# Elementwise work with two SBUF inputs moved from GpSimd to VectorE in a hybrid recurrence and MLP step

## The chip, the cores and the metric

The kernel runs on one core of a Trainium2 chip. The metric is device time in microseconds (us) of one execution. The engines are called as in the profile: PE is TensorE's matrix multiply, PEld its weight load, DVE is VectorE, ACT is ScalarE, POOL is GpSimd, SP is SyncE, which here only issues DMAs. Each engine runs its own instructions in the order of the program and waits on semaphores for the others.

## The reference

One inference step of a diffusion backbone with two layers over 128 context and 1024 latent tokens (1152 together), model width 1024, all in float32:

```python
for i in range(2):
    sh1, sc1, gt1, sh2, sc2, gt2 = adaln(cond, ada_w[i], ada_b[i])      # silu(cond) @ w + b
    h = rmsnorm(x, norm_mix_g[i]) * (1 + sc1) + sh1
    o = hgrn2_mixer(h, ...) if i == 0 else chunk_mlp_mixer(h, ...)
    x = x + gt1 * o
    h = rmsnorm(x, norm_mlp_g[i]) * (1 + sc2) + sh2
    x = x + gt2 * (square(relu(h @ w1)) @ w2)                           # hidden width 4096
y = rmsnorm(x, final_norm_g)

def hgrn2_mixer(h, ...):      # per head, both directions, 8 heads of 128
    zq, zff, zfb, zi, zg = split(h @ w_in);  q = silu(zq);  v = zi
    f = lb + (1 - lb) * sigmoid(zf);  k = 1 - f
    # S_t = f_t * S_(t-1) + k_t v_t^T,  o_t = S_t^T q_t
    o = rmsnorm(o_forward + o_backward) * silu(zg);  return o @ w_out, final states

def chunk_mlp_mixer(h, ...):  # chunks of 128 tokens, 8 groups
    u, v = split(gelu(h @ w_in));  v = layernorm(v)
    s = w_s @ v + b_s          # over the positions of a chunk
    return (u * s) @ w_out
```

The outputs are y of both token groups and the final states of the recurrence.

## The kernel before, in words

Tokens lie in the free dimension, in three blocks of TB = 384; the model width is 8 tiles of 128 partitions (KD = 8). A float32 product is done as three matmuls on a faster float32 form: a high part of each operand and the rest ("low part"), high x high, high x low, low x high (`mm3`). The high part of a weight is a copy by ACT, the low part is raw minus high, a `tensor_tensor` with two SBUF inputs on DVE or POOL (`hi_lo`, L241; each weight names its engine). Names: `wraw` is the loaded weight (128x1024, by SP's queue, two buffers for it and `adav` together), `whi`/`wlo` and `wunit` its parts, `hh`/`hl`, `hidh`/`hidl`, `hc`, `oh`/`ol`, `uh`/`ul` those of activations. Low parts are put in a list `late` and issued by `flush()`, in most places at once; weights are split ahead of use by `w_ahead()`.

The program is written out in one order; nothing reorders it. Its stages in the profiled execution are roughly: input norm and adaLN (0 to 110 us), the recurrence (110 to 740), head 7 beside the first half of the output projection (740 to 850), the second half, the first MLP's first token block and adaLN's end (to 1150), its other two blocks with Winograd's seven products in place of eight (`quad`, 1150 to 1655), the gMLP mixer (1655 to 2025), the second MLP and the final norm (2025 to 2823).

*Recurrence.* The program interleaves two generators: `z_groups(h)` multiplies the input projection of head h in 15 steps, here called slots (five sections times three token blocks), and `gla_gen(h - 1)` does the recurrence of the head before. In slot 0 lie ks, K and Q, in slot 1 the products aps, in slots 2 to 8 the seven levels, in 9 and 10 the transposes ktp, in 11 and 12 the state updates S with the products ups, in 13 and 14 the outputs og from the products ops; the gated norm (orp) of a head follows in the next head's slots 0, 2 and 3. K = 1 - F stands before ks. A level multiplies K and Q by decays (`L964`, `L971`, `L972` on DVE), forms the pairwise products of the decays for the next level (`TT`, `L962`, on POOL), does the products lps on PE and merges them under a mask (`L974` on DVE). The next level's lps reads this level's Q.

*adaLN.* The rest of the first layer's adaLN is a product of a vector with a matrix on DVE, in steps (`ada_vec`, L375): a tile `adav` of 512 KB is loaded, and a step does four multiply-and-accumulate instructions over half of it. The load of the next tile is issued by the generator behind the last read of a tile. Of the ring of two buffers that it shares with `wraw`, adav uses one and the same buffer each time in the recurrence. In the recurrence one step stands in each of slots 2 to 6 and 9 to 14. Two steps per quarter of the matrix only fill `bc`.

*Squares.* For the norms ACT squares each tile (`sq_step`) and the squares are added into `acc`, nearly all on POOL (L436); ones-matmuls then sum over partitions (`ss`, `rms_a`), DVE takes the reciprocal root (`rq`), a matmul spreads it (`rp`), ACT copies it to SBUF (`rstd`).

*Winograd.* A weight tile pair is loaded and summed: one sum on DVE (L292, to PSUM), three on POOL (L293, L298, L299, `SUM_ENG`); their low parts are on DVE.

Of the kernel before, what the change touches and what calls it, by code (L numbers as in the profile page):

```python
# [19 lines left out]
KD = 8  # L20
# [18 lines left out]
def kernel(  # L39
# [95 lines left out]
    for h in range(8):  # L135
        for sect in (3, 0, 1, 2, 4) if h == 0 else (4, 3, 0, 1, 2):
            plain(w_in[sect * 8 + h], [KD, 128], nc.gpsimd)
    for part in range(2):
        for p in range(4):
            plain(w_out[part, p], [2, 4, 128], nc.gpsimd)  # L140

    # Winograd's form of the 2 x 2 x 2 block product, seven block products in place of eight.  A: w1 transposed,
    # in blocks of (hidden, model); B: the normed tokens, in blocks of (model, token block 1 or 2).
    # S1 = A21 + A22, S2 = S1 - A11, S3 = A11 - A21, S4 = A12 - S2
    # T1 = B12 - B11, T2 = B22 - T1, T3 = B22 - B12, T4 = B21 - T2
    # C11 = A11 B11 + A12 B21, U = A11 B11 + S2 T2, C12 = U + S1 T1 + S4 B22,
    # C22 = U + S3 T3 + S1 T1, C21 = U + S3 T3 + A22 T4
    W_SPLIT = ("A11", "A12", "S1", "S2", "S4", "S3", "A22")

    def mlp_specs(l):  # L150
# [5 lines left out]
        for part in range(1, 2):  # L156
            engs = (SUM_ENG, nc.vector)
            for b in range(8):
# [10 lines left out]
                def unit(p):  # L169
                    for n2 in range(1 if tail else 2):  # L170
                        at["u", 2 * p + n2] = len(items)
                        add_item("plain" if tail else "unit", (down[p],), n2, nc.gpsimd if tail else nc.vector)

# [17 lines left out]
    UP += [(1, n) for n in ("A12", "S2", "S4", "S3")] + [("u", 0), ("u", 1), (1, "A22")]  # L191
    SUM_ENG = nc.gpsimd
    P0_ENG = nc.vector

    mlp_specs(0)
    for half in range(2):
        for kp in range(4):
            plain(cw_v[half, kp], [2, 512], nc.gpsimd if half == 0 else nc.vector)
    for g in range(8):
        plain(cw_u[g], [KD, 128], nc.vector)  # L200
    for n in range(8):
        plain(cw_out[n], [KD, 128], nc.vector if n < 4 else nc.gpsimd)
    mlp_specs(1)
# [126 lines left out]
    def w_ahead(depth=None, most=2):  # L330
        d = depth if depth is not None else (3 if wextra else 1)
        n = 0
        while wst["split"] < wst["use"] + d and n < most and w_split():
            n += 1

    def mm3(ps, wh, wl, act, n, k0=0, k1=None):
        for k in range(k0, n if k1 is None else k1):
            ah, al = act(k)
            nc.tensor.matmul(ps, wh(k), ah, start=(k == 0), stop=False)  # L339
            nc.tensor.matmul(ps, wh(k), al, start=False, stop=False)  # L340
            nc.tensor.matmul(ps, wl(k), ah, start=False, stop=(k == n - 1))  # L341
# [80 lines left out]

    def sq_step(j, k, eng=None):
        xs = xtiles[k][:, tbs(j)]
        if j not in accs:
            acc = (wextra[0] if wextra and j == 1 else scr).tile([128, TB], F32, tag="acc", name="acc", bufs=1)
            nc.scalar.activation(acc, xs, AF.Square)
            accs[j] = acc
        else:
            p, tag, n = sq_pool  # L430
            sq = p.tile([128, TB], F32, tag=tag, name="sq", bufs=n)
            nc.scalar.activation(sq, xs, AF.Square)
            if eng == "last":
                accs[j] = (accs[j], sq)
                return
            (eng or nc.gpsimd).tensor_tensor(out=accs[j], in0=accs[j], in1=sq, op=ALU.add)  # L436

    rstds = {}

    rq = {}  # L440
    n4 = TB // 4

    def rms_a(j):
        ss = psum.tile([128, n4], F32, tag="n", name="ss", bufs=1)
        parts = accs.pop(j)
        parts = parts if isinstance(parts, tuple) else (parts,)
        for x, acc in enumerate(parts):
            for b in range(4):
                nc.tensor.matmul(ss[32 * b:32 * b + 32], ones_d, acc[:, b * n4:(b + 1) * n4],
                                 start=(x == 0), stop=(acc is parts[-1]))  # L450
        q = scr.tile([128, n4], F32, tag="rq", name="rq", bufs=1)
        nc.scalar.activation(q, ss, AF.Sqrt, bias=eps_sb[:, 0:1])
        nc.vector.reciprocal(q, q)
        rq[j] = q

    def rms_b(j, pool=None, tag="rstd"):
# [6 lines left out]
        nc.scalar.activation(r, rp, AF.Copy)  # L463
        rstds[j] = r

    H = {}
# [77 lines left out]
    def tail_groups(bodies, make_norm, per_step, lag, per_w, js=range(NTB), queue=()):  # L544
        queue = list(queue)
        for i, j in enumerate(js):
            for n, body in enumerate(bodies):
# [5 lines left out]
                for _ in range(per_step):  # L553
                    qstep(queue)
                if i == 0 and n < per_w or j == js[-1]:
                    w_ahead()
        queue.append(make_norm(js[-1]))
        return queue

    HC = {}  # L560
    C1_POOL = ("B11", "B22", "B21")
    ADA_PACE = (0.65, 0.72)
# [9 lines left out]
    def comb1(i):  # L572
# [6 lines left out]
        def put(n, q, t):  # L579
# [8 lines left out]
            HC[1, n, q] = w  # L588
            hi_lo(w, t, nc.gpsimd if n in C1_POOL else nc.vector, mine)

# [77 lines left out]
    with tc.manual_schedule():  # L668
# [18 lines left out]
        with tc.tile_pool(name="start", bufs=14, reuse_waits="tile") as sp:  # L687
# [43 lines left out]

            def squares(j, eng):
                for k in range(KD):
                    sq_step(j, k, eng)

            def norms(j, k0, k1, sq=()):
                for _, k in zip(norm_gen(0, j, False, k0, k1), list(sq) + [None] * KD):
                    if k is not None:
                        sq_step(2, k, nc.gpsimd if k < 6 else nc.vector)

# [13 lines left out]
            a_load(2)  # L754
            squares(0, nc.vector)
            rms_a(0)
# [12 lines left out]
            w0s[0] = w_next()  # L769
            squares(1, nc.vector)  # L770
            sbs = a_mm(2)
# [35 lines left out]
        with tc.tile_pool(name="gla", bufs=1, reuse_waits="tile") as gla:  # L807
# [14 lines left out]
            def z_groups(h):  # L822
# [60 lines left out]
                for sect, j in seq:  # L883
# [13 lines left out]
                    if (sect == 0 and j == 2 or sect == 4) if h == 0 else j == 0:  # L897
                        w_ahead()
                    yield st
# [5 lines left out]
            def gla_gen(h, st):  # L905
# [7 lines left out]
                for j in range(NTB):  # L913
                    eng = nc.vector if h == 7 else nc.gpsimd
                    eng.tensor_scalar(out=K[:, :, tbs(j)], in0=F[:, :, tbs(j)], scalar1=-1.0, scalar2=1.0,
                                            op0=ALU.mult, op1=ALU.add)
# [34 lines left out]
                for lev in range(7):  # L951
# [10 lines left out]
                    nc.gpsimd.tensor_tensor(out=cut(Tn, t0n, [[1, n]]), in0=cut(Tcur, t0c, [[2, n]]),  # L962
                                            in1=cut(Tcur, t0c + 1, [[2, n]]), op=ALU.mult)
                    nc.vector.tensor_tensor(out=kmix(hh), in0=kview(km, hh),  # L964
# [6 lines left out]
                    nc.vector.tensor_tensor(out=q0, in0=q0, in1=cut(Tcur, t0c + n + 1, [[2, nb], [0, hh]]), op=ALU.mult)  # L971
                    nc.vector.tensor_tensor(out=q1, in0=q1, in1=cut(Tcur, t0c, [[2, nb], [0, hh]]), op=ALU.mult)  # L972
                    if lev < 5:
                        nc.vector.copy_predicated(A32, mask_sb[:, lev:lev + 1, :].to_broadcast([128, NC, 32]), pss[0])  # L974
# [92 lines left out]
            def split_og(h, j):  # L1067
                oh = ptile("oh")
                ol = ptile("ol")
                split(oh, ol, ogt[h][:, tbs(j)], nc.vector if h % 2 else nc.gpsimd)  # L1070
                OG[h, j] = (oh, ol)

            def out_group(part, w, np_, n2, j):
                ps = zps("wops")
                mm_p(ps, w, n2, lambda k: OG[4 * part + k, j])
                resid(0, 2, 2 * np_ + n2, j, ps)

            spare = []
            ada = ada_vec0(lambda: spare[0] if slot % 15 < 7 else spare[1])
# [3 lines left out]
            for h in range(8):  # L1083
                for st in z_groups(h):
                    step(prev)
                    step(cur)
                    if h > 0 and slot % 15 in (2, 3, 4, 5, 6, 9, 10, 11, 12, 13, 14):
                        step(ada)
# [18 lines left out]
            for np_ in range(4):  # L1107
                w = w_next()
                for n2 in range(2 if np_ < 3 else 1):
                    for j in range(NTB):  # L1110
# [3 lines left out]
                        if j == 0 and n2 == 0:  # L1114
                            w_ahead()
                        step(prev)
                        if j < 2 or n2 == 0 and np_ > 0 or np_ == 2:
                            step(cur)
                        if np_ == 1 and n2 == 0:
                            for h in range(4, 7):  # L1120
# [38 lines left out]
        def mlp(l, pend, make_norm, yp, ada, early):  # L1159
# [15 lines left out]
            def product(part, q, name, w, tick):  # L1175
# [156 lines left out]
            def t_body(np_, n2):  # L1332
                def f(j):
# [18 lines left out]
                    resid(l, 5, n, j, ps)  # L1352
                    sq_step(j, n, "last" if l == 1 and j == 2 and n == 7 else None)
                return f
# [76 lines left out]
        def gmlp2(gm, v):  # L1431
# [16 lines left out]
            def us_split(g, j):  # L1448
# [3 lines left out]
                nc.scalar.activation(uh.rearrange(c3, t=128), src, AF.Copy)  # L1452
                eng = nc.gpsimd if g % 4 == 3 else nc.vector
                eng.tensor_tensor(out=ul.rearrange(c3, t=128), in0=src, in1=uh.bitcast(F32).rearrange(c3, t=128),
                                  op=ALU.subtract)
# [63 lines left out]
        def final_gen(j):  # L1519
# [19 lines left out]
            yield  # L1539
            r = rstds.pop(j)  # L1540
            for k in sorted(range(KD), key=lambda k: (k - FPRE) % KD):
                if k in pre:
                    nc.gpsimd.tensor_tensor(out=pre[k], in0=pre[k], in1=r, op=ALU.mult)
                    y = pre[k]
                else:
                    y = out_tile()
                    nc.vector.scalar_tensor_tensor(out=y, in0=xtiles[k][:, tbs(j)], scalar=gain(k), in1=r,  # L1547
                                                   op0=ALU.mult, op1=ALU.mult)
# [72 lines left out]
```

## Time and profile before

| | |
|---|---|
| median of 3 runs | 2824.66 us (2823.97 to 2826.95) |
| span of the profiled execution | 2823.3 us |
| PE busy | 2713.9 us, 19696 instructions |
| DVE busy | 1771.7 us, 3674 instructions |
| ACT busy | 1201.6 us, 2116 instructions |
| POOL busy | 559.0 us, 422 instructions |
| DMA | 245.12 MB, mean 87 GB/s |

The profiled execution's span lies in the runs' spread a little under their lowest; all sums are made against it. A busy time is a sum of instructions; a matmul's row counts from issue to its modelled end, and neighbours overlap. In rows of the timeline the first two numbers are start and length, and `[1.68 <-DVE Q L972]` says that the engine stood idle for 1.68 us before the row, until that instruction of DVE released it. In tables of groups `x62 | 160.5, 2589` means 62 instructions, 160.5 us together, 2589 ns on average. In tables of windows the numbers are length, busy time and count of each engine, the clock granted to PE, and the DMA's share and GB/s.

### The profile page before, as it was taken

Reading aid. Unit: us, or ns where it says so; the run is one execution under the profiler, and the core shown is the slowest. Engines: PE = TensorE matmul, PEld = TensorE weight load, DVE = VectorE, ACT = ScalarE, POOL = GpSimd, SP = SyncE. Lnnn points to the kernel's source line nnn. Section 1 sums busy time; section 2 is a strip of 40 time slices with the busy share of each in tenths; the row PEclk is TensorE's granted clock in tenths of the full one; section 3 lists DMA queues with packets and bytes.
Section 4 is the critical chain, followed back from the end, with each engine's and each line's share of the span. In section 5 each row is a group of like instructions: output and inputs, shape, how many; then the busy total and the mean of one; then the engine's idle time right before and its main releaser. Section 6 shows DMA issues by size and latency. Waiting matters only on the chain. (4 is left out here: it accounts for less than half of the span.)

```text
span 2823.3 us, 48886 instructions
## 1 busy us (share of the span) xinstructions
PE 2713.9 (96%) x19696; PEld 2635.1 (93%) x19696; DVE 1771.7 (63%) x3674; ACT 1201.6 (43%) x2116; POOL 559.0 (20%) x422
## 2 busy tenths in 40 slices
PE   6999999999899999999999999999999999999998
PEld 4999999999889999999999987999999999999997
DVE  6267766677656886678888863433476565555554
ACT  4344434344335544543434463212454454434444
POOL 2232333323432100121111140002310012111113
PEclk8999999999999999999999999999999999999999
DMA  6112221212122445323333311111134332221221
GB/s 226 34 59 64 66 65 61 72 60 70 68 83 72 158 160 155 107 88 110 114 109 112 113 57 43 43 46 38 53 127 127 127 107 74 83 68 60 61 67 68
DMA packets 99874, 245.12 MB, mean 87 GB/s; under 512 B 11200, under 2 KB 50496, under 8 KB 99648
## 3 DMA queue, kind: packets, MB, share of 16 engines
q1 hardware_dynamic: 99648, 242.00, 26.6%
q8 instruction: 155, 2.54, 0.4%
q14 instruction: 71, 0.58, 0.1%
HBM read 236.19 MB, written 5.77 MB: 86 GB/s over the span
## 5 line engine op out<-in xcount | busy, mean ns | idle before, releaser
L526 DVE SCALAR_TENSOR_TENSOR x<-bps,mod,x 128x384 f32<-128x384 f32 (+2 forms) x512 | 248.7, 512 | 174.2 <-PE bps L341 173.5
L339 PE MATMUL zps<-hh,whi 128*128 128x384 f32 x912 | 318.6, 349 | 8.6 <-ACT hh L481 8.6
L1187 PE MATMUL quad<-hc,wunit 128*128 128x384 f32 x896 | 303.7, 339 | 11.6 <-ACT qt L1200 8.7
L340 PE MATMUL zps<-hl,whi 128*128 128x384 f32 x912 | 309.2, 339 | 3.9 <-DVE hl L489 3.5
L341 PE MATMUL zps<-hh,wlo 128*128 128x384 f32 x912 | 308.0, 338 | 0.0
L1189 PE MATMUL quad<-hc,wunit 128*128 128x384 f32 x896 | 303.2, 338 | 3.4 <-DVE wunit L241 3.4
L340 PE MATMUL bps<-hidl,wunit 128*128 128x384 f32 x896 | 301.9, 337 | 4.0 <-DVE hidl L241 3.9
L1188 PE MATMUL quad<-hc,wunit 128*128 128x384 f32 x896 | 302.2, 337 | 0.0
L339 PE MATMUL bps<-hidh,wunit 128*128 128x384 f32 x896 | 301.6, 337 | 0.0
L341 PE MATMUL bps<-hidh,wunit 128*128 128x384 f32 x896 | 301.3, 336 | 0.0
L238 ACT ACTIVATE wunit<-wraw 128x512 fp32r<-128x512 f32 x304 | 187.5, 624 | 247.9 <-PE bps L341 247.9
L238 ACT ACTIVATE whi<-wraw 128x1024 fp32r<-128x1024 f32 x206 | 216.9, 1053 | 121.8 <-DMA wraw<-w 81.5
L241 DVE TENSOR_TENSOR wunit<-wraw,wunit 128x512 fp32r<-128x512 f32 x304 | 222.7, 742 | 30.5 <-ACT wunit L238 30.1
L241 DVE TENSOR_TENSOR wlo<-wraw,whi 128x1024 fp32r<-128x1024 f32 x144 | 178.1, 1237 | 99.0 <-ACT whi L238 92.3
L293 POOL TENSOR_TENSOR wraw<-wraw 128x512 f32<-128x512 f32 x32 | 42.8, 1337 | 967.2 <-DVE s L292 821.6
L241 POOL TENSOR_TENSOR wlo<-wraw,whi 128x1024 fp32r<-128x1024 f32 x62 | 160.5, 2589 | 322.2 <-ACT whi L238 313.9
L241 DVE TENSOR_TENSOR hidl<-qt,hidh 128x384 fp32r<-128x384 f32 x192 | 110.4, 575 | 176.3 <-ACT hidh L238 176.0
L340 PE MATMUL bps<-hidl,whi 128*128 128x384 f32 x640 | 215.6, 337 | 2.6 <-DVE hidl L241 2.6
L339 PE MATMUL bps<-hidh,whi 128*128 128x384 f32 x640 | 216.3, 338 | 0.2 <-ACT hidh L238 0.2
L341 PE MATMUL bps<-hidh,wlo 128*128 128x384 f32 x640 | 215.4, 337 | 0.0
L375 DVE SCALAR_TENSOR_TENSOR junk<-adav,bc 128x256 f32<-128x256 f32 x384 | 191.0, 540 | 22.2 <-DMA adav<-ada_w 22.2
L339 PEld LDWEIGHTS zps<-hh,whi 128*128 128x128 f32 x912 | 172.7, 189 | 17.6 <-ACT hh L481 10.5
(225 smaller groups left out, 6508.0 us busy)
## 6 DMA issues: line engine op xcount, KB each, us to landing
wraw<-w SPq DMA_DIRECT2D x256, 512.0 KB, 3.6
adav<-ada_w SPq DMA_DIRECT2D x192, 128.0 KB, 2.2
wraw<-w_in SPq DMA_DIRECT2D x40, 512.0 KB, 3.7
adav<-ada_w SPq DMA_DIRECT2D x32, 512.0 KB, 3.6
adar<-ada_w SPq DMA_DIRECT2D x16, 512.0 KB, 8.3
x<-xT SPq DMA_DIRECT2D x24, 192.0 KB, 5.5
x<-xT SPq DMA_DIRECT2D x8, 576.0 KB, 4.1
yT<-y SPq DMA_DIRECT2D x24, 192.0 KB, 1.9
```

Source lines behind the costliest of these rows:

```text
L238: nc.scalar.activation(w[0], src, AF.Copy)
L241: eng.tensor_tensor(out=w[1], in0=src, in1=w[0].bitcast(F32), op=ALU.subtract)
L293: add.tensor_tensor(out=a21, in0=a11, in1=a21, op=ALU.subtract)
L339: nc.tensor.matmul(ps, wh(k), ah, start=(k == 0), stop=False)
L340: nc.tensor.matmul(ps, wh(k), al, start=False, stop=False)
L341: nc.tensor.matmul(ps, wl(k), ah, start=False, stop=(k == n - 1))
L375: nc.vector.scalar_tensor_tensor(out=junk_tile(), in0=raw[:, p], scalar=1.0, in1=bc[:, c * 256:(c + 1) * 256], op0=ALU.mult, op1=ALU.mult, ...
L526: nc.vector.scalar_tensor_tensor(out=xs, in0=ps[:, a:b], scalar=g, in1=xs, op0=ALU.mult, op1=ALU.add)
L1187: nc.tensor.matmul(p, w[0][:, k, :], bh, start=(first and k == 0), stop=False, **go)
L1188: nc.tensor.matmul(p, w[0][:, k, :], bl, start=False, stop=False, **go)
L1189: nc.tensor.matmul(p, w[1][:, k, :], bh, start=False, stop=(k == 3), **go)
```

## The change

Every `tensor_tensor` of POOL with two SBUF inputs goes to DVE: low parts of the recurrence's weights and of part of the others, the square sums, the sums of Winograd's weights, three of the low parts `hc`, TT, the low parts `ol` of even heads and a quarter of `ul`. On POOL stay the gates F (a `tensor_scalar` with one SBUF tile, L849), K = 1 - F, now for all eight heads (head 7's was on DVE), and three of the last y. With it:

- a square is added when the next one is issued, one later, and the last is summed by four more ones-matmuls (`rms_a`) in place of an addition;
- low parts and weight splits behind them are issued later (`w_ahead_late`, and `flush()` in every third slot, in the next group or after the next body);
- TT is issued behind the two Q operations of its level;
- the adaLN steps are dealt to the slots by a table, none in the levels, two in slots 9, 10, 13 and 14;
- the last block's y on DVE reads the spread reciprocal root from PSUM.

```diff
-            plain(w_in[sect * 8 + h], [KD, 128], nc.gpsimd)
+            plain(w_in[sect * 8 + h], [KD, 128], nc.vector)
...
-    SUM_ENG = nc.gpsimd
+    SUM_ENG = nc.vector
...
+    def w_ahead_late():
+        env["defer"] = True
+        w_ahead()
+        env["defer"] = False
...
-            if eng == "last":
-                accs[j] = (accs[j], sq)
-                return
-            (eng or nc.gpsimd).tensor_tensor(out=accs[j], in0=accs[j], in1=sq, op=ALU.add)
+            if len(accs[j]) == 2:
+                acc, old = accs[j]
+                nc.vector.tensor_tensor(out=acc, in0=acc, in1=old, op=ALU.add)
+            accs[j] = [accs[j][0], sq]
...
-            hi_lo(w, t, nc.gpsimd if n in C1_POOL else nc.vector, mine)
+            hi_lo(w, t, nc.vector, mine)
...
-                    eng = nc.vector if h == 7 else nc.gpsimd
-                    eng.tensor_scalar(out=K[:, :, tbs(j)], in0=F[:, :, tbs(j)], scalar1=-1.0, scalar2=1.0,
+                    nc.gpsimd.tensor_scalar(out=K[:, :, tbs(j)], in0=F[:, :, tbs(j)], scalar1=-1.0, scalar2=1.0,
...
-                    nc.gpsimd.tensor_tensor(out=cut(Tn, t0n, [[1, n]]), in0=cut(Tcur, t0c, [[2, n]]),
-                                            in1=cut(Tcur, t0c + 1, [[2, n]]), op=ALU.mult)
...
+                    nc.vector.tensor_tensor(out=cut(Tn, t0n, [[1, n]]), in0=cut(Tcur, t0c, [[2, n]]),
+                                            in1=cut(Tcur, t0c + 1, [[2, n]]), op=ALU.mult)
...
+            ADA_SLOTS = (1, 1, 0, 0, 0, 0, 0, 0, 0, 2, 2, 1, 1, 2, 2)
...
-                    if h > 0 and slot % 15 in (2, 3, 4, 5, 6, 9, 10, 11, 12, 13, 14):
+                    if slot % 15 % 3 == 1 or h == 0:
+                        flush()
+                    for _ in range(ADA_SLOTS[slot % 15] if h > 0 else 0):
                         step(ada)
...
+            rd = rps[j] if j == 2 else r
...
-                    nc.vector.scalar_tensor_tensor(out=y, in0=xtiles[k][:, tbs(j)], scalar=gain(k), in1=r,
+                    nc.vector.scalar_tensor_tensor(out=y, in0=xtiles[k][:, tbs(j)], scalar=gain(k), in1=rd,
```

Lines in the rows below are those of each file; the changed one's are 4 to 10 higher. DVE in the first two levels of a head, before:

```order
L964 TENSOR_TENSOR K<-km,F 128x576x2
L971 TENSOR_TENSOR Q<-Q,F 128x576
L972 TENSOR_TENSOR Q<-Q,F 128x576
L974 COPY_PREDICATED A_7006<-mask_sb,lps 128x288
L375 SCALAR_TENSOR_TENSOR A,mod<-adav,bc 128x256 x4
L1063 TENSOR_TENSOR og_5009<-og_5009,orp 128x288 x2
L964 TENSOR_TENSOR K<-km,TT 128x288x2x2
L971 TENSOR_TENSOR Q<-Q,TT 128x288x2
L972 TENSOR_TENSOR Q<-Q,TT 128x288x2
```

The same place in the changed kernel:

```order
L967 TENSOR_TENSOR K<-km,F 128x576x2
L974 TENSOR_TENSOR Q<-Q,F 128x576
L975 TENSOR_TENSOR Q<-Q,F 128x576
L976 TENSOR_TENSOR TT<-F 128x1152
L979 COPY_PREDICATED A_6036<-mask_sb,lps 128x288
L1068 TENSOR_TENSOR og_4029<-og_4029,orp 128x288 x2
L967 TENSOR_TENSOR K<-km,TT 128x288x2x2
L974 TENSOR_TENSOR Q<-Q,TT 128x288x2
L975 TENSOR_TENSOR Q<-Q,TT 128x288x2
L976 TENSOR_TENSOR TT<-TT 128x576
```

TT has come in behind Q, and the adaLN step (adav) has gone from the level.

DVE behind the last level of a head, before (a name's number tells its tile apart; S0 and S1 are the states of the two directions):

```order
L964 TENSOR_TENSOR K_4995<-km_5617,TT_4999 128x9x2x64
L971 TENSOR_TENSOR Q_4996<-Q_4996,TT_4999 128x9x64
L972 TENSOR_TENSOR Q_4996<-Q_4996,TT_4999 128x9x64
L375 SCALAR_TENSOR_TENSOR A32_4998,mod_79<-adav_5548,bc_4458 128x256 x8
L1017 SCALAR_TENSOR_TENSOR S0_5719<-S0_5719,TT_4999,ups_5817 128x128 x2
L1017 SCALAR_TENSOR_TENSOR S1_5721<-S1_5721,TT_4999,ups_5826 128x128 x3
```

and in the changed kernel:

```order
L975 TENSOR_TENSOR Q_5025<-Q_5025,TT_5028 128x9x64
L976 TENSOR_TENSOR TT_5028<-TT_5028 128x18
L380 SCALAR_TENSOR_TENSOR A32_5027,mod_79<-adav_5086,bc_4080 128x256 x4
L380 SCALAR_TENSOR_TENSOR A32_5027,mod_79<-adav_5752,bc_4080 128x256 x4
L241 TENSOR_TENSOR wlo_5727<-wraw_5640,whi_5726 128x1024
L380 SCALAR_TENSOR_TENSOR A32_5027,mod_79<-adav_5752,bc_4080 128x256 x4
L380 SCALAR_TENSOR_TENSOR A32_5027,mod_79<-adav_5807,bc_4080 128x256 x4
L1022 SCALAR_TENSOR_TENSOR S0_5729<-S0_5729,TT_5028,ups_5840 128x128 x2
L1022 SCALAR_TENSOR_TENSOR S1_5731<-S1_5731,TT_5028,ups_5849 128x128 x3
```

Where two steps stood ahead of the states, both on one tile, there are now four, on three tiles (5086, 5752, 5807), and a low part between them.

DVE in the Winograd stage, before (s is the sum in PSUM, qt a product's sum, hidl its low part):

```order
L241 TENSOR_TENSOR wunit<-wraw,wunit 128x512 x2
L292 TENSOR_TENSOR s_12482<-wraw 128x512
L1210 TENSOR_TENSOR qt<-quad,qt 128x384
L241 TENSOR_TENSOR wunit<-wraw,wunit 128x512 x2
L241 TENSOR_TENSOR hidl<-qt,hidh 128x384
L241 TENSOR_TENSOR wunit<-wraw,wunit 128x512
```

and in the changed kernel:

```order
L241 TENSOR_TENSOR wunit<-wraw,wunit 128x512 x2
L292 TENSOR_TENSOR s_12500<-wraw 128x512
L293 TENSOR_TENSOR wraw<-wraw 128x512
L1220 TENSOR_TENSOR qt<-quad,qt 128x384
L241 TENSOR_TENSOR wunit<-wraw,wunit 128x512 x2
L241 TENSOR_TENSOR hidl<-qt,hidh 128x384
L241 TENSOR_TENSOR wunit<-wraw,wunit 128x512
L298 TENSOR_TENSOR wraw<-wraw 128x512
L299 TENSOR_TENSOR wraw<-wraw 128x512
```

The three sums L293, L298 and L299 have come into DVE's order, one of them ahead of qt.

More of the change, by code (lines that the diff above doesn't have):

```diff
@@ L136 @@
         for sect in (3, 0, 1, 2, 4) if h == 0 else (4, 3, 0, 1, 2):
-            plain(w_in[sect * 8 + h], [KD, 128], nc.gpsimd)
+            plain(w_in[sect * 8 + h], [KD, 128], nc.vector)
     for part in range(2):
         for p in range(4):
-            plain(w_out[part, p], [2, 4, 128], nc.gpsimd)
+            plain(w_out[part, p], [2, 4, 128], nc.vector)
     W_SPLIT = ("A11", "A12", "S1", "S2", "S4", "S3", "A22")
@@ L171, in unit @@
                         at["u", 2 * p + n2] = len(items)
-                        add_item("plain" if tail else "unit", (down[p],), n2, nc.gpsimd if tail else nc.vector)
+                        add_item("plain" if tail else "unit", (down[p],), n2, nc.vector)
                 comb(0, W_SPLIT[:6])
@@ L197 @@
         for kp in range(4):
-            plain(cw_v[half, kp], [2, 512], nc.gpsimd if half == 0 else nc.vector)
+            plain(cw_v[half, kp], [2, 512], nc.vector)
     for g in range(8):
@@ L201 @@
     for n in range(8):
-        plain(cw_out[n], [KD, 128], nc.vector if n < 4 else nc.gpsimd)
+        plain(cw_out[n], [KD, 128], nc.vector)
     mlp_specs(1)
@@ L421, with sq_step @@
     sq_pool = [scr, "s", 4]
-    def sq_step(j, k, eng=None):
+    def sq_step(j, k):
         xs = xtiles[k][:, tbs(j)]
@@ L427, in sq_step @@
             nc.scalar.activation(acc, xs, AF.Square)
-            accs[j] = acc
+            accs[j] = [acc]
         else:
@@ L432, in sq_step @@
             nc.scalar.activation(sq, xs, AF.Square)
[L433 to L436 removed]
+            if len(accs[j]) == 2:
+                acc, old = accs[j]
+                nc.vector.tensor_tensor(out=acc, in0=acc, in1=old, op=ALU.add)
+            accs[j] = [accs[j][0], sq]
     rstds = {}
+    rps = {}
     rq = {}
@@ L445, in rms_a @@
         parts = accs.pop(j)
-        parts = parts if isinstance(parts, tuple) else (parts,)
         for x, acc in enumerate(parts):
@@ L464, in rms_b @@
         rstds[j] = r
+        rps[j] = rp
     H = {}
@@ L554, in tail_groups @@
                     qstep(queue)
+                flush()
                 if i == 0 and n < per_w or j == js[-1]:
-                    w_ahead()
+                    w_ahead_late()
         queue.append(make_norm(js[-1]))
@@ L730, in loads, with squares @@
                     nc.sync.dma_start(out=xtiles[k][:, tbs(j)], in_=xT[k, :, tbs(j)])
-            def squares(j, eng):
+            def squares(j):
                 for k in range(KD):
-                    sq_step(j, k, eng)
+                    sq_step(j, k)
             def norms(j, k0, k1, sq=()):
@@ L738, in norms @@
                     if k is not None:
-                        sq_step(2, k, nc.gpsimd if k < 6 else nc.vector)
+                        sq_step(2, k)
             w0s = {}
@@ L754 @@
             a_load(2)
-            squares(0, nc.vector)
+            squares(0)
             rms_a(0)
@@ L769 @@
             w0s[0] = w_next()
-            squares(1, nc.vector)
+            squares(1)
             sbs = a_mm(2)
@@ L897, in z_groups @@
                     if (sect == 0 and j == 2 or sect == 4) if h == 0 else j == 0:
-                        w_ahead()
+                        w_ahead_late()
                     yield st
@@ L1069, in split_og @@
                 ol = ptile("ol")
-                split(oh, ol, ogt[h][:, tbs(j)], nc.vector if h % 2 else nc.gpsimd)
+                split(oh, ol, ogt[h][:, tbs(j)], nc.vector)
                 OG[h, j] = (oh, ol)
@@ L1086 @@
                     step(cur)
-                    if h > 0 and slot % 15 in (2, 3, 4, 5, 6, 9, 10, 11, 12, 13, 14):
+                    if slot % 15 % 3 == 1 or h == 0:
+                        flush()
+                    for _ in range(ADA_SLOTS[slot % 15] if h > 0 else 0):
                         step(ada)
@@ L1114 @@
                         if j == 0 and n2 == 0:
-                            w_ahead()
+                            w_ahead_late()
                         step(prev)
@@ L1118 @@
                             step(cur)
+                        if j == 1:
+                            flush()
                         if np_ == 1 and n2 == 0:
@@ L1352, in f @@
                     resid(l, 5, n, j, ps)
-                    sq_step(j, n, "last" if l == 1 and j == 2 and n == 7 else None)
+                    sq_step(j, n)
                 return f
@@ L1452, in us_split @@
                 nc.scalar.activation(uh.rearrange(c3, t=128), src, AF.Copy)
-                eng = nc.gpsimd if g % 4 == 3 else nc.vector
-                eng.tensor_tensor(out=ul.rearrange(c3, t=128), in0=src, in1=uh.bitcast(F32).rearrange(c3, t=128),
+                nc.vector.tensor_tensor(out=ul.rearrange(c3, t=128), in0=src, in1=uh.bitcast(F32).rearrange(c3, t=128),
                                   op=ALU.subtract)
```

1 line of the change is left out of this document (removed).

## The prediction

> **What bounds the kernel now.** I read the page first, then TensorE's waits, then the stages in which these waits lie. The page's first part:
>
> ```profile
> PE 2713.9 (96%) x19696; PEld 2635.1 (93%) x19696; DVE 1771.7 (63%) x3674; ACT 1201.6 (43%) x2116; POOL 559.0 (20%) x422
> ```
>
> TensorE (PE) is busy for 2713.9 us of the 2823.3 us span. No matmul that counts is taken away, so all that the change can give is some of the 109.4 us in which PE stands still; what it can cost has no such limit. Which idle time is it? The table of waits (PE; for whom; us in total, times, longest):
>
> ```profile
> PE lps L933 <- DVE Q L972: 25.8, 16, 2.1
> PE ss L449 <- DVE acc L436: 10.9, 1, 10.9
> PE quad L1187 <- ACT qt L1200: 8.7, 6, 2.9
> PE zps L339 <- ACT hh L481: 8.6, 6, 4.0
> PE rp L460 <- DVE rq L453: 7.7, 6, 1.8
> PE bps L340 <- DVE hidl L241: 6.5, 7, 1.9
> PE vps L1388 <- POOL wlo L241: 2.0, 1, 2.0
> ```
>
> PE waits for GpSimd (POOL) itself in hardly any place. It waits for VectorE (DVE), and most often at the level products of the recurrence heads (lps waiting for Q). Why is Q late? One level of head 3 in the timeline, DVE, then POOL, then PE (start, length):
>
> ```profile
> 316.72 0.73 DVE L972 TENSOR_TENSOR Q<-Q,F 128x576 f32<-128x576 f32 x1
> ...
> 320.20 2.83 DVE L964 TENSOR_TENSOR K<-km,TT 128x1152 f32<-128x1152 f32 x1
> 322.95 1.70 DVE L971 TENSOR_TENSOR Q<-Q,TT 128x576 f32<-128x576 f32 x1
> 324.57 0.75 DVE L972 TENSOR_TENSOR Q<-Q,TT 128x576 f32<-128x576 f32 x1
> ...
> 327.33 1.35 DVE L964 TENSOR_TENSOR K<-km,TT 128x1152 f32<-128x1152 f32 x1
> ...
> 319.41 2.40 POOL L241 TENSOR_TENSOR wlo<-wraw,whi 128x1024 fp32r<-128x1024 f32 x1 [10.71 <-ACT whi L238]
> 321.77 2.27 POOL L962 TENSOR_TENSOR TT<-TT 128x576 f32<-128x576 f32 x1
> ...
> 318.25 0.83 PE L933 MATMUL lps<-Q,km 128*32 128x32 f32 x72
> 325.47 0.82 PE L933 MATMUL lps<-Q,km 128*32 128x32 f32 x72 [1.68 <-DVE Q L972]
> 343.28 0.82 PE L933 MATMUL lps<-Q,km 128*32 128x32 f32 x72 [1.69 <-DVE Q L972]
> ```
>
> K takes 1.35 us when POOL is still (327.33) and 2.83 us beside a low part on POOL; Q takes 1.70 instead of 0.75 beside the decay product TT. Each DVE operation that reads two SBUF tiles ends about when the POOL operation beside it ends: the two take turns. Then PE waits 1.68 us at level 2, and 1.69 us at level 5, of each of six heads: 6 x 3.37 = 20.2 us. The level slots have no room left, while the rest of the head has:
>
> ```profile
> 316.72:345.14 28.42, 27.10 (x61) 1.00 0.23 76
> ...
> 355.29:402.35 47.06, 25.68 (x76) 1.00 0.24 74
> ```
>
> These are windows of DVE alone (length, busy): 95% busy in the levels, and 21.4 us idle of 47.06 between a head's last level and the next head's first.
>
> **The change, part by part.** Prices of the moved work (line, engine; count; busy us, mean ns):
>
> ```profile
> L241 POOL TENSOR_TENSOR wlo<-wraw,whi 128x1024 fp32r<-128x1024 f32 x62 | 160.5, 2589 | 322.2 <-ACT whi L238 313.9 <-DVE q L829 7.8 <-DVE hidl L241 0.5
> L241 DVE TENSOR_TENSOR wlo<-wraw,whi 128x1024 fp32r<-128x1024 f32 x144 | 178.1, 1237 | 99.0 <-ACT whi L238 92.3
> L436 POOL TENSOR_TENSOR acc<-acc,sq 128x384 f32<-128x384 f32 x88 | 96.8, 1100 | 166.4 <-ACT sq L432 165.1 <-PE rp L460 0.6
> L241 DVE TENSOR_TENSOR hidl<-qt,hidh 128x384 fp32r<-128x384 f32 x192 | 110.4, 575 | 176.3 <-ACT hidh L238 176.0
> L293 POOL TENSOR_TENSOR wraw<-wraw 128x512 f32<-128x512 f32 x32 | 42.8, 1337 | 967.2 <-DVE s L292 821.6
> L241 DVE TENSOR_TENSOR wunit<-wraw,wunit 128x512 fp32r<-128x512 f32 x304 | 222.7, 742 | 30.5 <-ACT wunit L238 30.1
> ```
>
> Onto DVE come some 64 low parts at 1.24 us (79), 74 square sums at 0.58 (43), 96 Winograd sums at 0.74 (71), 24 low parts of hc at 0.58 (14) and eight heads' TT products (1.35, then 0.75 and halving, about 3.4 a head: 27), with some 10 us of og and u: about 244 us of new work, less what the lengthened operations give back. DVE stays under three quarters busy in total, so it doesn't become the bound as a whole; the question is where.
>
> *Levels.* Each loses an ada step (four products over adav) and its lengthening, and gains TT behind Q. From Q at 316.72 to Q at 324.57 now lie 7.85 us, 1.74 of an ada step, 1.48 of lengthened K and 0.95 of lengthened Q; TT at 1.35 comes in. That gives about 5 us, inside PE's level slot of 325.47 - 1.68 - 318.25 = 5.5 us. Both waits go: -20.2.
>
> *The ada steps that left the levels.* They now stand in the eight slots around the levels, two to a slot in four of them. One step:
>
> ```profile
> 332.03 0.08 DVE L375 DVE_READ_ACCUMULATOR A<-adav,bc 128x1 f32 x1
> ...
> 332.14 0.33 SPq L389 DMA_DIRECT2D adav<-ada_w  x1
> ...
> 335.93 0.42 DVE L375 SCALAR_TENSOR_TENSOR A<-adav,bc 128x256 f32<-128x256 f32 x1 [0.81 <-DMA adav<-ada_w]
> ...
> 337.67 0.55 DVE L829 TENSOR_TENSOR q<-zps,sig 128x384 f32<-128x384 f32 x1
> ```
>
> A step is 335.93 to 337.67, 1.74 us, and takes half a tile. The next tile's load goes out only when the last half of the old one has been read (332.14, 0.11 after its end) and DVE can start on it 3.8 us later. Today a slot's other work covers this: 0.81 us was waited here. In the new order a double step is nearly always the second half of one tile and the first half of the next, with nothing between, so DVE, which runs in order, stands 3.8 us in mid-slot. I count 20 such places in six heads (3, 3, 4, 3, 3, 4). Behind them are queued S, og, ks and Q, on which PE's state products, aps and lps hang.
>
> The budget of one window between levels: 64 half-tile steps lie in the six windows after, about 34 of them before, so 30 x 1.74 / 6 = 8.7 us more; three low parts 3.7; three stalls 11.4 or four 15.2. Against the 21.4 us idle DVE is 2.4 or 6.2 us late at the first level. PE's lps at 318.25 starts 0.8 us after the Q it needs (316.72 + 0.73), so PE waits 1.6 us in four heads and 5.4 us in two: 17 us. The lower end is 0, if the loads land while DVE would stand anyway for ScalarE or PE; the upper end is 36, if half the idle time is tied to PE's pace and can't be filled. I take 17, since every row of the budget is measured. Levels and ada together: -3 (from -20 to +16).
>
> *740 to 850, head 7 beside the first half of the output projection*, and the *first MLP with its Winograd sums* (windows: length, PE busy, PEld busy, DVE busy, ACT busy, POOL busy), then one place of the latter:
>
> ```profile
> 740.00:850.00 110.00, 95.85 (x1059) 90.44 (x1059) 74.56 (x121) 40.61 (x71) 45.40 (x30) 0.95 0.24 85
> ...
> 1150.00:1655.00 505.00, 488.22 (x2765) 482.99 (x2764) 397.17 (x1007) 226.63 (x435) 84.60 (x62) 0.99 0.33 104
> ...
> 1365.02 1.63 POOL L298 TENSOR_TENSOR wraw<-wraw 128x512 f32<-128x512 f32 x1 [1.63 <-issue]
> ...
> 1365.42 1.52 DVE L375 SCALAR_TENSOR_TENSOR junk<-adav,bc 128x256 f32<-128x256 f32 x1
> ...
> 1371.42 0.45 PE L1187 MATMUL quad<-hc,wunit 128*128 128x384 f32 x1 [2.88 <-ACT qt L1200]
> ```
>
> In the first, PE idles 14.2 us. POOL's 45.4 us turn into some 22 on a DVE that has 35 free, but its levels are as short as DVE's own work there: +1 (-5 to +5). In the second, PE idles 16.8 us. DVE, 79% busy, gets the sums; a sum of 0.74 replaces about 1.1 us of lengthening (1.52 where 0.42 is usual), so DVE's load is about level and the work is spread. The 2.88 us wait ends such a chain: DVE late, qt late. I take a third of the idle time: -6 (-10 to +3).
>
> *The rest.* At the start, low parts on DVE end sooner than on POOL: -2 (-5 to 0); the 10.9 us wait of ss is for the input and stays. POOL's low part before vps (2.0) and its neighbours: -2.5. hidl beside POOL's low parts in the two MLP tails, two waits of 0.8: -1.6. The second MLP: -0.5. The last square is never added but goes through PE: eight records more, 14 times. The end of the kernel has all three rows:
>
> ```profile
> 2810.31 0.37 PE L449 MATMUL ss<-sq,ones_d 128*32 128x96 f32 x8 [0.45 <-ACT sq L432]
> ...
> 2813.16 0.49 ACT L463 ACTIVATE rstd<-rp 128x384 f32<-128x384 f32 x1 [0.56 <-ACT y L1534]
> 2813.68 5.04 DVE L1547 SCALAR_TENSOR_TENSOR y<-x,vec_sb,rstd 128x384 f32<-128x384 f32 x5 [1.79 <-ACT rstd L463]
> 2813.73 3.52 POOL L1543 TENSOR_TENSOR y<-y,rstd 128x384 f32<-128x384 f32 x3 [4.29 <-ACT rstd L463]
> ```
>
> 14 x 0.37 is 5 us at most; they overlap and end a sum that was late: +4. Reading the reciprocal root from PSUM skips the 0.49 us copy, and y no longer takes turns with POOL (5.04 for five; 0.58 each by hidl's mean would be 2.9, but three POOL results and the stores still follow): -1.7 (-3 to 0). A low part one group later stays ahead of its use, as ScalarE's copy and the load were early; SP's next weight load waits for that read, but weights are split a group ahead: 0 (0 to +5). K of head 7 on POOL reads one SBUF tile: 0.
>
> Sum: -20.2 + 17 + 1 - 6 - 2 - 2.5 - 1.6 - 0.5 + 4 - 1.7 = -12.5. From the profiled 2823.3 us span this is 2811; the median of the runs shown stands 1.4 us above that span, so 2812.
>
> **The rivals.** *The ada stalls are covered* (loads land in idle time, 0 instead of 17): 2795. For it: DVE idles 21.4 us a window. Against: the budget above has already given that whole idle time to the added work, and it doesn't reach. *The stalls take the time back*, and this one ends slower: if DVE's idle time there is tied to PE's pace, 36 instead of 17, and Winograd's part 1 finds DVE full (+3 instead of -6): 2812 + 19 + 9 = 2840; with the stalls alone 2831. It decides when a head's first levels start over 3.4 us later than now (20.2 / 6). For it: DVE runs in order and the stall comes ahead of ks. *The stalls slow PE's clock as well*. The trace has one stretch in the heads where PE waited repeatedly and the granted clock (first number behind the busy time) fell:
>
> ```profile
> 752.00:764.00 12.00, 9.91 (x176) 0.72 0.58 229
> ```
>
> If the two 5.4 us stalls brought the same 0.72 over 12 us, that is 3.4 us each, and the time is 2819. The Trainium skill, "TensorE: Matmul & The Clock Gate", Part 1 (The HAM clock gate), says that an idle window of about 3.4 us halves the clock; by that rule the two long stalls trip it and the four short ones don't. This trace agrees only in part: the clock fell here although I see no wait that long in this stretch. *The change doesn't do what it says* (GpSimd's gates and K, which stay, lengthen DVE as before): against it, the levels' POOL rows are TT and low parts alone; 2823, with little chance.
>
> **How the numbers follow.** Forecast, stalls of 10 to 25 us: 2804 to 2820, chance 0.42. Covered, 2790 to 2804: 0.18. Clock as well, or little gained, 2819 to 2830: 0.2. Slower, 2830 to 2850: 0.2. A measurement here can tell about 0.2% (5.6 us). Below 2819: most of the first and all of the second, 0.54; within 2819 to 2830: 0.23; above: 0.23. The range leaves out a tenth on each side: 2793 to 2838.
>
> **What would show it.** DVE's K and Q at 1.35 and 0.75 everywhere in the levels, and no lps wait at levels 2 and 5. DVE waiting for adav, some 20 times about 3.8 us, in the slots behind the levels; PE waiting at aps or the first lps. No wide POOL rows. PE's sum over 1150 to 1655 a few us shorter. I am wrong if lps waits stay at their old levels, if S or og after a double step holds PE up in every head, or if a new wait for wlo or wunit appears in the MLPs.

## The result and the profile after

The changed kernel takes 2874.2 us (median of 4 runs, 2873.28 to 2874.77) against 2825.25 us before: ratio 1.0173, 95% interval 1.0159 to 1.0188. The forecast was 2812, with 2793 to 2838 as range. It is slower by 49 us. The row of engines from its page:

```profile
PE 2737.2 (95%) x19808; PEld 2651.8 (92%) x19808; DVE 1835.3 (64%) x4003; ACT 1201.1 (42%) x2116; POOL 57.8 (2%) x79
```

PE's waits (for whom; us in total, times, longest), and DVE's for adav:

```profile
PE lps L938 <- DVE A L979: 30.5, 7, 5.0
PE aps L938 <- DVE ks L923: 18.3, 7, 4.3
PE orp L1065 <- DVE og L1068: 8.6, 6, 2.8
PE ups L1010 <- DVE S L1022: 5.3, 9, 1.1
PE lps L938 <- DVE Q L975: 2.6, 2, 2.1
```

```profile
DVE A L380 <- DMA adav<-ada_w: 102.7, 28, 5.0
```

POOL has lost 501 us of work and DVE gained only 64, where the forecast put 244 us of new work onto it: what the lengthened operations gave back pays for most of the move. The waits of lps for Q fell from 25.8 to 2.6 us. But in the recurrence DVE now waits 102.7 us for adav (18 before), and PE waits for what stands behind that: ks, the mask A, og, S. Where the 49 us lie follows from the first instruction of each stage (first and last start in the groups by tile):

| from, to | before | after | difference |
|---|---|---|---|
| start, first ks | 125.7 | 121.5 | -4.2 |
| first ks, ks of head 7 (recurrence) | 619.6 | 679.6 | +60.0 |
| ks of head 7, first quad | 411.8 | 413.1 | +1.3 |
| first quad, first vps (Winograd) | 531.8 | 528.4 | -3.4 |
| first vps, last cops (gMLP) | 335.5 | 330.1 | -5.4 |
| last cops, end | 798.9 | 799.5 | +0.6 |

So everything but the recurrence gave 11 us, and the recurrence took 60. One head of it, in the timeline of DVE, SP and PE:

```profile
327.81 0.42 DVE L380 SCALAR_TENSOR_TENSOR A<-adav,bc 128x256 f32<-128x256 f32 x1 [4.30 <-DMA adav<-ada_w]
336.60 1.36 DVE L967 TENSOR_TENSOR K<-km,TT 128x1152 f32<-128x1152 f32 x1
337.86 0.76 DVE L974 TENSOR_TENSOR Q<-Q,TT 128x576 f32<-128x576 f32 x1
...
371.23 0.42 DVE L380 SCALAR_TENSOR_TENSOR A<-adav,bc 128x256 f32<-128x256 f32 x1
375.42 0.42 DVE L380 SCALAR_TENSOR_TENSOR A<-adav,bc 128x256 f32<-128x256 f32 x1 [3.75 <-DMA adav<-ada_w]
384.83 0.42 DVE L380 SCALAR_TENSOR_TENSOR A<-adav,bc 128x256 f32<-128x256 f32 x1 [4.73 <-DMA adav<-ada_w]
394.73 0.42 DVE L380 SCALAR_TENSOR_TENSOR A<-adav,bc 128x256 f32<-128x256 f32 x1 [1.74 <-DMA adav<-ada_w]
406.34 0.42 DVE L380 SCALAR_TENSOR_TENSOR A<-adav,bc 128x256 f32<-128x256 f32 x1 [4.45 <-DMA adav<-ada_w]
414.10 0.42 DVE L380 SCALAR_TENSOR_TENSOR A<-adav,bc 128x256 f32<-128x256 f32 x1 [3.69 <-DMA adav<-ada_w]
...
371.69 0.33 SPq L394 DMA_DIRECT2D adav<-ada_w  x1
...
336.13 1.19 PE L938 MATMUL lps<-Q,km 128*32 128x32 f32 x72 [4.72 <-DVE A L979]
417.33 0.86 PE L938 MATMUL aps<-q,ks 128*32 128x32 f32 x72 [4.13 <-DVE ks L923]
```

K and Q have their undisturbed lengths, 1.36 and 0.76. But between 371 and 415 DVE stands five times for a tile: the load goes out at 371.69, when the old tile's last read is over, and DVE starts on it at 375.42. A sixth time comes in the next slot 1 (here 327.81, of this head). Two windows of DVE, between the same operations as the two of the kernel before (levels, and the stretch between levels), show the shift (length, busy):

```profile
333.58:359.69 26.11, 18.30 (x29) 0.89 0.07 22
369.85:431.39 61.54, 36.74 (x121) 0.97 0.27 84
```

The levels, 27.1 us busy of 28.4 before, are now 18.3 of 26.1, so 2.3 us shorter; the stretch between, 47.06 long before, has grown to 61.5.

### The profile page after: what moved, and what is told of

Same layout as the page of the kernel before. It is cut to its first block, busy times and chain, and to the rows that moved or that the text cites. A ratio compares the mean times of both kernels' runs of the same rounds, so it can differ in the third digit from the quotient of the medians.

```text
span 2872.2 us, 48679 instructions
## 1 busy us (share of the span) xinstructions
PE 2737.2 (95%) x19808; PEld 2651.8 (92%) x19808; DVE 1835.3 (64%) x4003; ACT 1201.1 (42%) x2116; POOL 57.8 (2%) x79
## 4 chain that ended last, share of the span: by engine, by line
PE 74%; DVE 14%; DMA 6%; ACT 4%; issue 2%; SPq 0%; POOLq 0%; POOL 0%; DVEq 0%; ACTq 0%
PE bps L345 8%; PE bps L346 8%; PE bps L344 8%; DMA adav<-ada_w 4%; PE quad L1197 4%; PE quad L1199 4%; PE quad L1198 4%; PE zps L344 3%; PE zps L345 3%; PE zps L346 3%; PE aps L346 3%; PE aps L345 3%; PE aps L344 3%; DVE A L380 3%; PE ups L344 1%
## 5 line engine op out<-in xcount | busy, mean ns | idle before, releaser
L241 DVE TENSOR_TENSOR wlo<-wraw,whi 128x1024 fp32r<-128x1024 f32 x206 | 251.4, 1220 | 101.9 <-ACT whi L238 101.3
L241 DVE TENSOR_TENSOR wunit<-wraw,wunit 128x512 fp32r<-128x512 f32 x304 | 205.7, 686 | 25.8 <-ACT wunit L238 25.8
L1197 PEld LDWEIGHTS quad<-hc,wunit 128*128 128x128 f32 x896 | 169.3, 189 | 16.7 <-ACT qt L1210 9.8
L345 PEld LDWEIGHTS zps<-hl,whi 128*128 128x128 f32 x912 | 176.9, 194 | 5.3 <-DVE hl L495 5.2
L346 PEld LDWEIGHTS zps<-hh,wlo 128*128 128x128 f32 x912 | 176.3, 193 | 2.8 <-DVE wlo L241 2.8
```

Of the source, the lines that this page charges most:

```text
L241: eng.tensor_tensor(out=w[1], in0=src, in1=w[0].bitcast(F32), op=ALU.subtract)
L1197: nc.tensor.matmul(p, w[0][:, k, :], bh, start=(first and k == 0), stop=False, **go)
```

## The experiments

A number in us is the median of a kernel's runs, beside the kernel before on the same chip; `after` is the changed kernel. ADA is its table of adaLN steps by slot. Runs 1 to 4, 5 to 8 and 9 to 12 were taken on three chips, on which the kernel before took 2824.0, 2824.9 and 2824.0 us; the runs of one kernel spread over some 1 to 12 us, so a difference of 2 or 3 us between two runs says nothing.

**1 to 4: is it the adaLN steps, and their tiles?** First the parity alone.

```diff
-                    for _ in range(ADA_SLOTS[slot % 15] if h > 0 else 0):
+                    for _ in range(ADA_SLOTS[slot % 15] + (slot == 15) if h > 0 else 0):
```

> The changed kernel with one adaLN step more in slot 0 of head 1, so that from there each double step is both halves of one adav tile and not the second half of one and the first half of the next. Theory A (VectorE stands in mid-slot for the next adav tile; 102.7 us of such waits in the changed kernel's trace): the waits for adav in the recurrence fall below 45 us, since the load goes out at a slot's end, and the time falls to 2815 to 2840. Rival B (the added work in VectorE's order is too much around the levels: low parts, TT ahead of the mask, ada steps in fewer slots): nothing of that is changed, 2860 to 2875.

2823.0 us against 2824.0 before (ratio 0.9996, 0.9986 to 1.0006). One step more at the start, with all other work as in `after`, takes 51 us off. The waits for adav fall to 30.1 us. A holds, B falls.

```diff
-            ADA_SLOTS = (1, 1, 0, 0, 0, 0, 0, 0, 0, 2, 2, 1, 1, 2, 2)
+            ADA_SLOTS = (1, 1, 0, 0, 0, 1, 1, 1, 1, 1, 1, 1, 1, 1, 1)
```

> The changed kernel with the same 12 adaLN steps a head dealt one to a slot: slots 0, 1 and 5 to 14. Theory A: waits for adav below 30 us in the recurrence, the time 2800 to 2822, under the kernel before. Rival B: the same VectorE work, two steps of it now in the levels 3 and 4: 2855 or more.

2826.2 us (1.0006, 0.9995 to 1.0017): the stalls are gone as expected (29.8 us left), but the time is not under the kernel before; this expectation missed. The slots 0 and 1 show why (DVE, PE, and a window of all engines, whose clock is the number behind the last busy time):

```profile
316.90 0.42 DVE L380 SCALAR_TENSOR_TENSOR A<-adav,bc 128x256 f32<-128x256 f32 x1 [2.04 <-DMA adav<-ada_w]
324.63 0.45 DVE L979 COPY_PREDICATED A<-mask_sb,lps 128x288 f32<-128x288 uint8 x1
...
325.23 1.19 PE L938 MATMUL lps<-Q,km 128*32 128x32 f32 x72 [4.55 <-DVE A L979]
```

```profile
321.00:333.00 12.00, 7.77 (x136) 7.54 (x139) 9.67 (x13) 4.01 (x5) 0.00 (x0) 0.72 0.01 1
```

Two steps ahead of the first level, with a wait for adav before the second, make its mask late. PE's next lps waits for that mask, 4.55 us here and 28.7 us in seven times, and the granted clock falls to 0.72 over the 12 us around it.

```diff
-            ADA_SLOTS = (1, 1, 0, 0, 0, 0, 0, 0, 0, 2, 2, 1, 1, 2, 2)
+            ADA_SLOTS = (0, 0, 1, 1, 1, 1, 1, 0, 0, 1, 1, 1, 1, 1, 1)
```

> The changed kernel with the adaLN steps in the slots of the kernel before (2 to 6, 9 to 14, one each). Theory A: waits for adav near the 18 us of before, but the first levels hold K, Q, TT and a step, some 6.8 us against PE's 5.5: PE waits 1 to 1.5 us in two or three levels a head, 2820 to 2845. Rival B: 2860 or more.

2804.9 us (0.993, 0.9914 to 0.9946): 69 us less than `after`, and 15 us better than the lower end that A gave it. The waits for adav are 11.7 us, those of lps for the mask 10.6 and for Q 7.9.

```diff
 (the kernel before)
-                    if h > 0 and slot % 15 in (2, 3, 4, 5, 6, 9, 10, 11, 12, 13, 14):
+                    for _ in range((1, 1, 0, 0, 0, 0, 0, 0, 0, 2, 2, 1, 1, 2, 2)[slot % 15] if h > 0 else 0):
```

> The kernel before with nothing changed but the slots of the adaLN steps (those of the changed kernel, with its double steps). Theory A: the stalls come although no work has moved between engines: 2850 to 2880, waits for adav of 80 to 110 us in the recurrence. Rival B: the time stays within 2815 to 2835, as the levels are relieved of steps and nothing is added.

2891.8 us (1.024, 1.0225 to 1.0255): without any work moved between engines, the table alone costs 68 us, 12 more than A's upper end. DVE waits 105.6 us for adav.

**5: steps clear of the first levels.** `ADA_SLOTS = (0, 0, 0, 1, 1, 1, 1, 1, 1, 1, 1, 1, 1, 1, 1)` in `after`.

> The changed kernel with 12 adaLN steps a head in slots 3 to 14, one each, none in slots 0 to 2. Theory A2 (two costs: VectorE's waits for adav, and steps ahead of the first level, which make its mask late so that PE stands 4 to 5 us a head and its clock falls): the waits of lps for the mask fall from 28.7 us (one step a slot in 0, 1 and 5 to 14) to below 13, and the time is 2795 to 2808. Rival B2 (12 steps outside the levels 0 and 1 are themselves too many): 2815 to 2830.

2799.1 us (0.9906, 0.9891 to 0.9921), the waits for the mask 10.6. Against run 2 only the slots differ, and it is 27 us: A2 holds. The table's 69 to 75 us are thus 51 for halves of two tiles in one slot, and 18 to 24 that runs 2 and 5 lay on the steps ahead of the first level. Within the latter the late mask and the shorter waits for adav (29.8 us in run 2, 20.8 in run 5) were not told apart.

**6 to 8: what did the move itself bring?** All three on run 3 (2804.9 us). In the first TT is issued behind the mask:

```diff
-                    nc.vector.tensor_tensor(out=cut(Tn, t0n, ...   # ahead of the mask
                     if lev < 5:
                         nc.vector.copy_predicated(A32, ...
...
+                    nc.vector.tensor_tensor(out=cut(Tn, t0n, ...   # behind it
                     Tcur, t0c = Tn, t0n
```

> As the run with the slots of the kernel before, but the decay product TT of a level issued behind the mask and not ahead of it. If TT ahead of the mask holds the next lps up (it frees a buffer in PSUM 1.35 us later in level 0), 3 to 10 us come off: 2795 to 2802. If not, the time is that of the old slots, within 3 us of 2805.

2802.6 us (0.9917, 0.99 to 0.9934): within the runs of 2804.9. The waits for the mask fall from 10.6 to 3.7 us, those for Q rise from 7.9 to 14.1. Whichever comes first, DVE's level is as long.

`SUM_ENG = nc.gpsimd`:

> As the run with the slots of the kernel before, but Winograd's 96 weight sums back on GpSimd. The prediction's term for the Winograd stages was 6 us of gain from moving them: 2808 to 2815 if it holds, with junk and wunit rows lengthened to 1.5 us again. If the sums' place is worth nothing: within 3 us of 2805.

2806.1 us (0.9931, 0.9916 to 0.9946). The junk rows (adaLN's products in this stage) lengthen again, from 445 to 522 ns in the mean, as expected. The Winograd stage is 530.2 us in this profile and 525.9 in run 3's, but the times don't differ beyond their spread: at most some 4 us of the 6 forecast.

```diff
-            plain(w_in[sect * 8 + h], [KD, 128], nc.vector)
+            plain(w_in[sect * 8 + h], [KD, 128], nc.gpsimd)
...
+                    nc.gpsimd.tensor_tensor(out=cut(Tn, t0n, [[1, n]]), in0=cut(Tcur, t0c, [[2, n]]),
+                                            in1=cut(Tcur, t0c + 1, [[2, n]]), op=ALU.mult)
                     nc.vector.tensor_tensor(out=kmix(hh), in0=kview(km, hh),
```

(and TT no longer on VectorE)

> As the run with the slots of the kernel before, but the low parts of the recurrence's input weights and the decay products TT back on GpSimd, as in the kernel before (TT ahead of K), while everything else stays on VectorE. If the two engines taking turns is what made PE wait in the levels, the waits of lps for Q come back (20 to 26 us) and the time is 2815 to 2828. If the gain of the old slots lay elsewhere: within 4 us of 2805.

2787.5 us (0.9869, 0.9852 to 0.9886). It went the other way: with the low parts and TT back on POOL the kernel is 17 us faster, the fastest of all. The lps waits for Q are 6.6 us and did not come back. So my reason for them was wrong, or not the whole of it.

**9 to 12: the engine, or the time of issue?** What run 8 still has of the change in the recurrence is the later issue of the low parts, and of the next weight's load that stands behind them. That alone, in the kernel before:

```diff
-                        w_ahead()
+                        w_ahead_late()
...
+                    if slot % 15 % 3 == 1 or h == 0:
+                        flush()
                     if h > 0 and slot % 15 in (2, 3, 4, 5, 6, 9, 10, 11, 12, 13, 14):
```

> The kernel before, every operation on the engine it had, with one thing changed: in the recurrence a weight's low part and what hangs behind it is issued in the next slot (slots 1, 4, 7, 10, 13; in head 0 every slot) and not at once. Theory C (what made PE wait in the levels is when the low part stands in GpSimd's order, ahead of the TT of levels 1 and 4, and not that the two engines take turns): the lps waits for Q fall from 25.8 to below 12 us and the time is 2800 to 2812. Rival D (the engine is what matters): 2820 to 2830.

2804.1 us against 2824.0 (0.9924, 0.9912 to 0.9936). Every operation is on the engine that it had, and the lps waits for Q fall from 25.8 to 4.3 us. C holds. The reverse is run 8 with the low parts issued at once (`w_ahead()` in the slots, no `flush()` there):

> As the run with low parts and TT of the recurrence back on GpSimd, but with those low parts issued at once, as in the kernel before. Theory C: the lps waits for Q come back, 18 to 26 us, and the time rises from 2788 to 2802 to 2815. Rival D: within 5 us of 2788.

2811.2 us (0.995, 0.9934 to 0.9966), 24 more than run 8, and the lps waits for Q are back at 26.3 us. C holds both ways. POOL, DVE and PE at levels 1 and 2, in run 10 and then in run 9:

```profile
316.16 2.40 POOL L241 TENSOR_TENSOR wlo<-wraw,whi 128x1024 fp32r<-128x1024 f32 x1 [10.73 <-ACT whi L238]
318.52 2.26 POOL L967 TENSOR_TENSOR TT<-TT 128x576 f32<-128x576 f32 x1
316.94 2.83 DVE L969 TENSOR_TENSOR K<-km,TT 128x1152 f32<-128x1152 f32 x1
319.70 1.70 DVE L976 TENSOR_TENSOR Q<-Q,TT 128x576 f32<-128x576 f32 x1
322.22 0.82 PE L938 MATMUL lps<-Q,km 128*32 128x32 f32 x72 [1.68 <-DVE Q L977]
```

```profile
304.19 1.24 POOL L967 TENSOR_TENSOR TT<-TT 128x576 f32<-128x576 f32 x1
319.04 2.39 POOL L241 TENSOR_TENSOR wlo<-wraw,whi 128x1024 fp32r<-128x1024 f32 x1
315.58 1.35 DVE L969 TENSOR_TENSOR K<-km,TT 128x1152 f32<-128x1152 f32 x1
320.44 2.20 DVE L969 TENSOR_TENSOR K<-km,TT 128x1152 f32<-128x1152 f32 x1
319.10 0.83 PE L938 MATMUL lps<-Q,km 128*32 128x32 f32 x72
```

In run 10 (as in the kernel before) the low part stands in POOL's order ahead of level 1's TT, and POOL stands 10.73 us until ACT has made that low part's `whi`. So TT, which could have run slots earlier, is pushed beside that level's K and Q, and both POOL operations lengthen them. In run 9 the TT of 576 is done at 305.4, ten us ahead of its level, K takes 1.35, and the low part falls in the next level, where it lengthens one K to 2.20 and nothing more. The engines take turns in both; only in the first is the level over its slot.

From the first ks to head 7's, run 8 takes 599.6 us and run 9 598.4 (619.6 before): the recurrence is as long in both. The 17 us between them lie in the other stages (Winograd 522.8 us against 533.1, gMLP 328.8 against 334.4), where the rest of the change, the moved work and its later issue together, does pay.

The last two are on run 8. ADA in slots 3 to 14:

> As the run with low parts and TT of the recurrence back on GpSimd, with 12 adaLN steps in slots 3 to 14. On VectorE alone these slots were worth 6 us; here VectorE has room in the levels, so 0 to 6: 2781 to 2790, the best of all if they add up.

2793.6 us (0.9888, 0.9875 to 0.9902): 6 us more, outside what I expected. The waits for adav are 23.8 us there and 13.3 in run 8; whether they are the cause I did not try. And TT alone on POOL, the low parts on VectorE:

> As the run with the slots of the kernel before, with TT alone back on GpSimd and the low parts left on VectorE. It splits the 17 us between 2805 and 2788: TT takes 3.4 us a head off VectorE and stands ahead of the mask, the low parts 6 us a head. If TT counts, 2790 to 2796; if the low parts, 2799 to 2805.

2794.1 us (0.9888, 0.9875 to 0.9902), in the range for TT: of run 3's 17 us some 11 are TT, and some 6 or 7 the low parts, near the least that these runs can tell.

## Why the prediction was wrong

*What bounds the kernel.* Right: PE's idle time was all there was to win, and DVE's total (64%) never became the bound.

*The level waits, -20.2.* The waits went, and the late issue alone takes 20 us off (run 9). My reason was half right. The operations do take turns, though not as I read the rows: K, beside the low part, ends 1.22 us after the low part's end (323.03, 321.81), TT 1.01 after K's end, Q 0.61 after TT's, each a little under its own undisturbed length (1.35, 1.24, 0.75) after the other engine's operation was over. But the move was not needed to cure the waits: with the low parts late, TT and low parts are better off on POOL (run 8), and on DVE they cost 17 us. What the move alone would do, with the low parts issued at once, no run shows. I had put the late issue at 0 (0 to +5); on POOL it was worth 20 to 24, and I never asked what it does to POOL's order. Had I looked at it, the row of TT behind the low part at 321.77 was there, 2.27 us long where run 9 has 1.24.

*The adaLN stalls, +17.* This is the step that failed: the term was the whole of what the table would cost, and runs 3 and 5 put that cost at 69 to 75 us. Mechanism and price of one stall were right: 3.8 us forecast, 102.7 / 28 = 3.7 measured. Three things in the working were wrong.

The count: I put down 20 stalls where 28 came, since the single steps in slots 12 and 1 wait too (1.74 and 4.30 above).

The reserve: I set all of DVE's 21.4 us of idle time between the levels against the new work and the stalls. In head 3's stretch DVE is busy for 11.1 us more than before (36.74 - 25.68) and waits 17.6 us more for adav (five waits, 18.36 us, where 0.76 was waited). Of the 20.6 us of other idle time 6.4 stay, so about two thirds took up work and a third did not, and the stretch grew by 14.5 us, where the forecast had 2.4 or 6.2. Why a third stayed I only read from the rows: that idle time is waiting for ACT and PE, and when S or og is late, what DVE waits for next is late as well.

The place: I let DVE's lateness reach PE once a head, at the first lps. PE waited in four places, for the mask, ks, og and S (30.5 + 18.3 + 8.6 + 5.3 = 62.7 us), and a step costs more ahead of the first level than elsewhere (run 2 against run 5, 27 us).

How much of a stall reaches the end, run 1 tells: it changes the alignment alone, DVE waits 72.6 us less for adav (102.7 - 30.1), and the kernel is 51 us faster, about seven tenths. In the kernel before, the table costs 68 us for 87 us more of such waits (105.6 - 18.2), with the steps ahead of the first level in it. The room that the steps left in the levels (8 us a head idle) isn't used either: in the levels DVE waits for PE's lps (20.4 us in all) and for ACT's sigmoids.

*The clock rival.* I gave it 7 us. In `after` PE is busy for 2737.2 us, in run 5, with the same matmuls, for 2712.8. This row is of `after`, and the stall of 4.72 us lies in it (length, PE busy, clock):

```profile
324.00:336.00 12.00, 4.57 (x26) 0.86 0.19 68
```

I read the 24 us as the lower clock, since PE's records lengthen with it (lps behind the stall 1.19 us, 0.83 elsewhere): about a third of the 75 us between the two kernels, so this was a part of the slow case and no case of its own. No run changes the clock alone. In run 5, with waits of that size nearly gone, the granted clock is 1.00 over the whole recurrence; in `after` it is 0.96. The rule of the Trainium skill, "TensorE: Matmul & The Clock Gate", Part 1 (The HAM clock gate), that an idle window of about 3.4 us costs clock, agrees with the stalls of 4 to 5 us here; it leaves the 0.72 that the kernel before shows at 752 to 764 us unexplained.

*The slower rival.* It named this mechanism and had 0.2; its 2840 rested on half of DVE's idle time being unfillable and on a loss in the Winograd stage that did not come. In head 3 a third stayed unfilled; what it lacked were the stalls of the single steps and the further places where PE waits, and 2874 lies outside its 2830 to 2850 as well.

*The rest.* From the table: start -4.2 (forecast -2), head 7 and the first MLP's start +1.3 (+1), Winograd -3.4 (-6), gMLP -5.4 (-2.5). The second MLP with the extra ones-matmuls and the end: +0.6 (-0.5, half of -1.6, +4 and -1.7, about +1). Together -11 against some -9, which is closer than most of the terms are: their misses partly cancel.

## What to carry to other kernels

Idle time of an engine that runs in order is no reserve to be spent in a lump: a third of it could not be filled in the head shown, and work ahead of something that PE needs is paid at once. Count as hidden only what stands in front of a wait that outlasts it, at that place. Work that reads a single-buffered tile and issues the next load itself may appear once per load latency; put two reads of different tiles side by side and the engine stands for the whole transfer. And before work is moved off an engine because it disturbs another, move it in the order of its own engine first: here that alone brought 20 us, and the best kernel (2787.5 us, 1.3% under the one before) keeps the recurrence's low parts and TT on GpSimd, issues the low parts a slot later, leaves the adaLN steps in the old slots, and moves the rest of the work to VectorE.

## What the runs showed of the hardware

A single wait of PE of 4 to 5 us goes with a granted clock of 0.72 to 0.86 over the 12 us around it; the two waits of 1.7 us a head that stood in the recurrence before left it at 1.00. DVE's part of the move was cheap in busy time: 501 us less on POOL came with 64 us more on DVE, since the same operations take about half as long there (1220 ns for a low part, 2589 on POOL before) and no longer stretch each other.
